# A two-layer fp32 block on one core: the last feed-forward multiplies both parts of x in one 512-column product

## The chip, the cores and the metric

The kernel runs on one core of a Trainium2 chip. The metric is the device time of one execution in microseconds, the median of several runs. The core's engines work side by side, each through its own queue in order: TensorE (PE; its weight loads have a row of their own, PEld), VectorE (DVE), ScalarE (ACT), GpSimd (POOL) and SyncE (SP, which issues the DMA transfers). They meet at semaphores.

## The reference

The reference is a two-layer model, then a second two-layer model on its output, all in fp32, with 256 tokens (272 with 16 meta tokens in front) and a width of 1024. What the change touches is one feed-forward, the last of the first model (layer 1, `ffn2`), on 256 tokens:

```python
D_MODEL, SEQ, D_FF = 1024, 256, 2816

def swiglu(h, w_gu, w_down):
    g, u = jnp.split(h @ w_gu, 2, axis=-1)
    return (jax.nn.silu(g) * u) @ w_down

f = swiglu(rms_norm(h, ln_ffn2[i, 0]), ffn2_w_gu[i], ffn2_w_down[i])
h = h + 0.5 * rms_norm(f, ln_ffn2[i, 1])
```

Around it stand three other feed-forwards (on 272 tokens), a convolution mixer and an attention mixer before it, and a recurrent and another attention mixer after it.

## The kernel before

**Layout.** Features lie on the partitions, tokens in the columns. The hidden state H is 8 tiles (KT) of 128 features by 272 tokens. A weight is a block of 128 x 128.

**Split products.** Products are made in fp32r. To keep fp32 accuracy each operand is split in a high part, rounded to fp32r, and a low part, the remainder: `xh`, `xl` for x, `hh`, `hl` for the hidden layer, `wh`, `wl` for the weights. `mm3` makes three products per weight into the same columns of a PSUM bank: wh x xh (line 290), wh x xl (line 291), wl x xh (line 292). In the last feed-forward each has 256 columns, half a bank.

**Weights.** All weights come from one stream (`Weights`): 201 DMA transfers of 16 blocks, issued by SP. A unit is 8 blocks. For each unit ACT casts the raw blocks to `wh` (line 160, 6 buffers) and VectorE subtracts to make `wl` (line 165, 5 buffers). `take` hands out block after block; at the first block of unit u it issues the cast of unit u + 4 and the subtraction of unit u + 3, so these stand in the queues of ACT and VectorE at that place. The order of instructions on each engine is the order of the program.

**The feed-forward (`ffn`).** The gate and the up projections have 22 column tiles (FT) each. Each is one `dense` call of 8 weights, that is one unit. The first four (gate and up of j = 0 and 1) are made together by `dense_group`, weight row by weight row, because x still arrives from the preceding boundary, one feature tile after another. Then the loop over j = 2 to 21: product pg (gate, in a bank `acc`), a step of side work, product pu (up, in a bank `m`), then `part1(j)` and `part2(j - 1)`:

- `part1`: VectorE multiplies pg by r (the inverse norm) to `f1`; ACT takes silu of it to `f2`; POOL multiplies `f2` by r.
- `part2`: VectorE multiplies `f2` by pu to `f3`; ACT copies that to `hh`; VectorE subtracts to make `hl`.

At j = 2 the parts of j = 0 and 1 come too, in the order part1(0), part1(1), part2(0), part1(2), part2(1). After the loop ACT loads another table, and part2(21) follows. The first two of `part1`, `part2` read PSUM on VectorE (rows `f<-acc` and `f<-f,m`).

**Side work.** `side_step` advances a modulation computed from `ada_w_2`: in one step POOL multiplies a piece `aw` of 1024 columns by `cond`, in the next ACT sums it. In this feed-forward it runs up to about j = 17.

**Down.** Eight products of 22 weights each (`dense` with `hh`, `hl`). `post_tile` takes each: ACT squares it for the norm (`sq`) and copies it scaled (`fs`), POOL adds up the squares. Then `boundary` sums the squares by a product with ones and makes the next x, with idle bf16 products (`warm`, line 287) in between.

PSUM has four banks with tag `acc` and four with `m`.

Of the kernel before, what the change touches and what calls it, by code (L numbers as in the profile page):

```python
# [10 lines left out]
F32R = mybir.dt.float32r  # L11
BF16 = mybir.dt.bfloat16
U32 = mybir.dt.uint32
AF = mybir.ActivationFunctionType
# [4 lines left out]
P = 128  # L19
D = 1024  # L20
KT = D // P
NMETA = 16
T = 272
TX = 256
DFF = 2816
FT = DFF // P
# [6 lines left out]
ROW = 320  # L33

AT = {"x1": 16, "h1": 0, "xc": 16, "x2": 12, "h2": 4, "x3": 20, "h3": 48, "xa": 16, "x4": 0, "h4": 0, "xe": 16, "xo": 16}
# [156 lines left out]
def build(tc, nc, ap, stop=99):  # L192
    V, A, G, PE, S = nc.vector, nc.scalar, nc.gpsimd, nc.tensor, nc.sync
    mult, add, sub = ALU.mult, ALU.add, ALU.subtract
# [4 lines left out]
    def tt(e, out, a, b, op):  # L199
        e.tensor_tensor(out=out, in0=a, in1=b, op=op)  # L200
# [10 lines left out]
    def table(f):  # L211
        if f in sets and loaded[0] != sets[f]:
            loaded[0] = sets[f]
            A.preload_act_table_set(sets[f])

    def act(out, a, f, **k):
        table(f)
        A.activation(out=out, in_=a, func=f, **k)  # L218
# [3 lines left out]
    with glob as gp, psp as ps, tc.tile_pool(name="tmp", bufs=2) as tp, tc.manual_schedule():  # L222

        def acc(tag="acc"):
            return ps.tile([P, 512], F32, tag=tag, name=tag)
# [4 lines left out]
        def tmp(tag, n=T, dt=F32, bufs=2, pool=None):  # L230
            return (pool or tp).tile([P, n], dt, tag=tag, name=tag, bufs=bufs)
# [2 lines left out]
        cv = gp.tile([P, CV.n], F32, name="cv")  # L234
        ct = gp.tile([P, CT.n], F32, name="ct")
        H = gp.tile([P, KT, T], F32, name="H")
        xparts = [gp.tile([P, KT * ROW], F32R, name=n) for n in ("xh", "xl")]
        xh = xl = None

        def rows(t, a, n):  # L240

            return t.rearrange("p (k t) -> p k t", t=ROW)[:, :, a : a + n]

        def place_x(a):
            nonlocal xh, xl
            xh, xl = (rows(t, a, T) for t in xparts)

        fs = bp.tile([P, KT, T], F32, name="fs")
        W = Weights(nc, gp, ap["wst"])
# [32 lines left out]
        def warm(n):  # L282

            if n:
                p = acc("m")
                for _ in range(n):
                    PE.matmul(p[:, :256], idle[:, :P], idle, start=True, stop=True)

        def mm3(out, w, a, b, start, stop):
            PE.matmul(out, w[0], a, start=start, stop=False)  # L290
            PE.matmul(out, w[0], b, start=False, stop=False)  # L291
            PE.matmul(out, w[1], a, start=False, stop=stop)  # L292
# [121 lines left out]
        def post_tile(st, p, k, tok, gpost):  # L414
            st.add(p, k == KT - 1)
            act(fs[:, k, tok], p, AF.Copy, scale=gpost[:, k : k + 1])

        def boundary(st, tok, gpre, last=False, prologue=False, dst=None, at=None):
            if at is not None:
                place_x(at)  # L420
# [64 lines left out]
        def pre_rstd(pre, n, direct=False):  # L485
            return rstd(pre.sums(), n, D, 1e-6, eps6, tag="rpre", direct=direct)

        active = []

        def slot():  # L490
            for g in list(active):
                if next(g, 1) == 1:
                    active.remove(g)

        def dense(keys, rhs, n, tag="acc"):

            p = acc(tag)[:, :n]
            for k, key in enumerate(keys):
                a, b = rhs(k)
                mm3(p, W.take(key), a, b, k == 0, k == len(keys) - 1)  # L500
                if k == 3 and active:
                    slot()
            return p

        def dense_group(keysets, rhs, n, order=None, tags=("acc",) * 4):

            pl = [acc(tags[i])[:, :n] for i in range(len(keysets))]
            nk = len(keysets[0])
            order = order or list(range(nk))
            for i, k in enumerate(order):  # L510
                a, b = rhs(k)
                if i:
                    for p, keys in zip(pl, keysets):
                        mm3(p, W.take(keys[k]), a, b, False, i == nk - 1)
                else:

                    ws = [W.take(keys[k]) for keys in keysets]
                    for part in range(2):
                        for p, w in zip(pl, ws):
                            PE.matmul(p, w[part], a, start=part == 0, stop=False)  # L520
                    for p, w in zip(pl, ws):
                        PE.matmul(p, w[0], b, start=False, stop=False)
                if active:
                    slot()
            return pl

        def xrhs(tok):
            return lambda k: (xh[:, k, tok], xl[:, k, tok])

# [10 lines left out]
        def side_step():  # L540
            if side:
                try:
                    next(side[0])
                except StopIteration:
                    side.popleft()


        def ffn(i, name, tok, pre, gpost, between=None, at=0):
            n = tok.stop - tok.start
            with tc.tile_pool(name="ffn", bufs=1) as fp:  # L550
                hh, hl = (rows(fp.tile([P, FT * ROW], F32R, name=m), at, n) for m in ("hh", "hl"))
                gu = lambda half, j: [(f"{name}_w_gu", i, k, half * FT + j) for k in range(KT)]
                x = xrhs(tok)
                state = {}

                def part1(j, pg, pu):
                    t1 = tmp("f1", pool=bp)[:, :n]
                    tt(V, t1, pg, r, mult)
                    s = tmp("f2", pool=bp)[:, :n]
                    act(s, t1, AF.Silu)  # L560
                    tt(G, s, s, r, mult)
                    state[j] = (s, pu)

                def part2(j):
                    s, pu = state.pop(j)
                    hid = tmp("f3", pool=bp)[:, :n]
                    tt(V, hid, s, pu, mult)
                    act(hh[:, j], hid, AF.Copy)
                    tt(V, hl[:, j], hid, hh[:, j].bitcast(F32), sub)

                first = dense_group([gu(0, 0), gu(1, 0), gu(0, 1), gu(1, 1)], x, n, tags=("acc", "m", "acc", "m"))
                for j in range(2, FT):
                    pg = dense(gu(0, j), x, n)
                    if i or name == "ffn2" or j >= 8:
                        side_step()
                    if j == 2:
                        r = pre_rstd(pre, n, True)
                    pu = dense(gu(1, j), x, n, "m")
                    if j == 2:
                        part1(0, first[0], first[1])  # L580
                        part1(1, first[2], first[3])
                        part2(0)
                    part1(j, pg, pu)
                    part2(j - 1)
                if between is None:
                    table(ARS)
                part2(FT - 1)
                st = Stats(n)
                for m in range(KT):
                    if m == 1 and between:  # L590
                        between()
                        table(ARS)
                    p = dense([(f"{name}_w_down", i, k, m) for k in range(FT)], lambda k: (hh[:, k], hl[:, k]), n)
                    if m == KT - 1:
                        W.ahead()
                    post_tile(st, p, m, tok, gpost)
                    if m < KT - 1:
                        side_step()
                return st
# [14 lines left out]
        def conv(pre):  # L614
            tok = slice(0, T)
            with tc.tile_pool(name="conv", bufs=1) as cp:
                oh, ol = (rows(cp.tile([P, KT * ROW], F32R, name=m), 0, T) for m in ("oh", "ol"))
                ub = [cp.tile([P, T + 2], F32, name=f"ub{j}") for j in range(2)]
                for u in ub:
# [235 lines left out]
        x2 = lambda k: (xh[:, k, :N2], xl[:, k, :N2])  # L855
# [515 lines left out]
        full, tok = slice(0, T), slice(NMETA, T)  # L1371
# [103 lines left out]
def program(stop=99):  # L1475
    import concourse.bacc as bacc

    nc = bacc.Bacc("TRN2", target_bir_lowering=False, num_devices=1)
    shapes = {
        "xT": (P, KT, T),  # L1480
        "cvec": (P, CV.n),
        "ctab": (P, CT.n - P),
        "ctab2": (P, CT2.n),
        "ada": (2, 24, P, D),
        "crep": (P, D),
        "poolw": (P, 4, P),
        "wst": (NCHUNK, P, SUB * P),
    }
    ap = {n: nc.dram_tensor(n, s, F32, kind="ExternalInput").ap() for n, s in shapes.items()}
    ap["out"] = nc.dram_tensor("out", (P, KT, TX), F32, kind="ExternalOutput").ap()  # L1490
    with tile.TileContext(nc) as tc:
        plan = build(tc, nc, ap, stop)
    return nc, plan
# [11 lines left out]
```

## Time and profile before

| | us |
|---|---|
| median of 3 runs | 1362.07 |
| lowest, highest | 1360.29, 1367.23 |
| the profiled execution's own time | 1369.89 |
| its span, first to last instruction | 1367.9 |

| engine | busy us | share of the span |
|---|---|---|
| PE | 1326.6 | 97% |
| PEld | 1288.2 | 94% |
| DVE | 1037.2 | 76% |
| ACT | 753.7 | 55% |
| POOL | 497.0 | 36% |

The mean granted TensorE clock is 0.993 of full speed. Matmuls are pipelined in the profile: the duration of one (0.28 us) is longer than the distance to the start of the next, so the pace of PE is read from starts. L290 is line 290 of the kernel before; `acc<-xh,wh` means that `acc` is written and `xh` and `wh` are read. The helpers at lines 197, 200, 204, 206 and 218 hold most VectorE, POOL and ACT operations, so rows are told apart by their tiles. The last feed-forward runs from 877.94 to 1068.3 us of the span; its loop over j ends about 1006.

### The profile page before, as it was taken

The page shows a single profiled execution, that of the slowest core. Times are in us where ns is not written, and L with a number is a line of the kernel's source. Part 1 is how long each engine was busy: PE and PEld are TensorE (multiplying, and loading weights), DVE is VectorE, ACT ScalarE, POOL GpSimd, SP SyncE. Part 2 cuts the span into 40 slices and gives each one's busy share as a digit, 9 for nine tenths or more (in the row PEclk, how much of TensorE's full clock was granted, in tenths as well). Part 3 has the DMA queues.
Part 4 walks back from the last instruction along what each step waited for, and adds up shares of the span by engine and source line. Part 5 has one row for each costly group of instructions (what it writes and reads, how often), then busy time and mean ns, then how long its engine had stood idle before and what let it go on. Part 6 is the DMA issues. An engine that isn't in the chain of part 4 may idle for free.

```text
span 1367.9 us, 25743 instructions
## 1 busy us (share of the span) xinstructions
PE 1326.6 (97%) x10458; PEld 1288.2 (94%) x10458; DVE 1037.2 (76%) x1505; ACT 753.7 (55%) x1314; POOL 497.0 (36%) x460
## 2 busy tenths in 40 slices
PE   8999999999999999999999998999999989999998
PEld 8999998998999998999998887899999889899888
DVE  6778558878898547988647877788854797877885
ACT  6555544455565545655545555665654546657663
POOL 2133223444333223432224775443200347523420
PEclk9999999999999999999999999999999999999999
DMA  7666663563666562676652332356655332454321
GB/s 251 241 225 221 227 216 97 209 209 133 214 249 231 217 216 109 216 246 207 218 194 95 139 105 93 124 200 240 229 210 185 129 124 97 153 183 155 124 93 62
DMA packets 39286, 242.23 MB, mean 177 GB/s; under 512 B 4352, under 2 KB 5888, under 8 KB 13696
## 3 DMA queue, kind: packets, MB, share of 16 engines
q1 hardware_dynamic: 39168, 240.59, 50.5%
q8 instruction: 82, 1.34, 0.4%
q14 instruction: 36, 0.29, 0.1%
HBM read 239.53 MB, written 1.05 MB: 176 GB/s over the span
## 4 chain that ended last, share of the span: by engine, by line
PE 73%; DVE 17%; POOL 5%; ACT 2%; issue 2%; DMA 0%; SPq 0%; POOLq 0%; ACTq 0%; DVEq 0%
PE acc L291 16%; PE acc L290 16%; PE acc L292 16%; PE m L292 7%; PE m L290 7%; PE m L291 7%; DVE wl L165 4%; DVE H L200 2%; DVE xl L197 1%; POOL rs L200 1%; DVE bt L197 1%; DVE ex L204 1%; POOL hx L200 1%; ACT wh L160 1%; DVE ev L200 1%
## 5 line engine op out<-in xcount | busy, mean ns | idle before, releaser
L165 DVE TENSOR_TENSOR wl<-raw,wh 128x1024 fp32r<-128x1024 f32 x400 | 587.8, 1492 | 132.9 <-ACT wh L160 75.1
L160 ACT CAST wh<-raw 128x1024 fp32r<-128x1024 f32 x400 | 407.1, 1041 | 46.5 <-PE acc L291 21.5
L290 PE MATMUL acc<-xh,wh 128*128 128x272 f32 (+2 forms) x1361 | 400.2, 294 | 2.7 <-ACT wh L160 1.9
L291 PE MATMUL acc<-xl,wh 128*128 128x272 f32 (+2 forms) x1361 | 393.2, 289 | 1.8 <-DVE xl L197 1.7
L292 PE MATMUL acc<-xh,wl 128*128 128x272 f32 (+2 forms) x1361 | 389.4, 286 | 0.6 <-DVE wl L165 0.6
L291 PEld LDWEIGHTS acc<-xl,wh 128*128 128x128 f32 x1361 | 259.6, 191 | 11.0 <-DVE xl L197 7.9
L290 PEld LDWEIGHTS acc<-xh,wh 128*128 128x128 f32 x1361 | 258.9, 190 | 8.5 <-issue 2.2
L292 PEld LDWEIGHTS acc<-xh,wl 128*128 128x128 f32 x1361 | 259.0, 190 | 1.0 <-DVE wl L165 0.9
L292 PE MATMUL m<-xh,wl 128*128 128x272 f32 (+2 forms) x855 | 245.2, 287 | 1.3 <-DVE wl L165 1.2
L290 PE MATMUL m<-xh,wh 128*128 128x272 f32 (+2 forms) x855 | 246.3, 288 | 0.0
L291 PE MATMUL m<-xl,wh 128*128 128x272 f32 (+2 forms) x855 | 244.7, 286 | 0.0
L290 PE MATMUL acc<-hh,wh 128*128 128x272 f32 (+1 forms) x704 | 201.9, 287 | 0.0
L291 PE MATMUL acc<-hl,wh 128*128 128x272 f32 (+1 forms) x704 | 201.9, 287 | 0.0
L292 PE MATMUL acc<-hh,wl 128*128 128x272 f32 (+1 forms) x704 | 201.9, 287 | 0.0
L200 POOL TENSOR_TENSOR sacc<-sacc,sq 128x272 f32<-128x272 f32 (+1 forms) x92 | 83.8, 911 | 291.9 <-ACT sq L218 274.3
L200 POOL TENSOR_TENSOR f<-f,rpre 128x272 f32<-128x272 f32 (+1 forms) x88 | 67.2, 765 | 315.6 <-ACT f L218 315.6
L292 PEld LDWEIGHTS m<-xh,wl 128*128 128x128 f32 x855 | 161.8, 189 | 2.0 <-DVE wl L165 1.9
L291 PEld LDWEIGHTS m<-xl,wh 128*128 128x128 f32 x855 | 162.4, 190 | 0.3
L290 PEld LDWEIGHTS m<-xh,wh 128*128 128x128 f32 x855 | 161.9, 189 | 0.3
L218 ACT ACTIVATE f<-f 128x272 f32<-128x272 f32 (+1 forms) x88 | 37.3, 428 | 180.7 <-DVE f L200 180.7
L291 PEld LDWEIGHTS acc<-hl,wh 128*128 128x128 f32 x704 | 133.6, 190 | 0.0
L292 PEld LDWEIGHTS acc<-hh,wl 128*128 128x128 f32 x704 | 132.9, 189 | 0.0
(377 smaller groups left out, 2062.8 us busy)
## 6 DMA issues: line engine op xcount, KB each, us to landing
raw<-wst SPq DMA_DIRECT2D x199, 1024.0 KB, 4.9
aw<-ada SPq DMA_DIRECT2D x48, 512.0 KB, 5.7
raw<-wst SPq DMA_DIRECT2D x3, 512.0 KB, 8.8
out<-H SPq DMA_DIRECT2D x8, 128.0 KB, 1.9
H<-xT SPq DMA_DIRECT2D x3, 272.0 KB, 8.0
raw<-wst SPq DMA_DIRECT2D x2, 256.0 KB, 3.6
cond<-crep SPq DMA_DIRECT2D x1, 512.0 KB, 5.7
cnt<-ctab SPq DMA_DIRECT2D x1, 512.0 KB, 3.7
```

Source lines behind the costliest of these rows:

```text
L160: self.nc.scalar.copy(self.h[u], r)
L165: self.nc.vector.tensor_tensor(out=self.l[u], in0=r, in1=self.h[u].bitcast(F32), op=ALU.subtract)
L197: V.scalar_tensor_tensor(out=out, in0=a, scalar=s, in1=b, op0=op0, op1=op1, **k)
L200: e.tensor_tensor(out=out, in0=a, in1=b, op=op)
L204: e.tensor_scalar(out=out, in0=a, scalar1=s1, scalar2=None, op0=op0)
L218: A.activation(out=out, in_=a, func=f, **k)
L290: PE.matmul(out, w[0], a, start=start, stop=False)
L291: PE.matmul(out, w[0], b, start=False, stop=False)
L292: PE.matmul(out, w[1], a, start=False, stop=stop)
```

## The change

In the feed-forward whose two parts fit in 512 columns (`pair`: 2 x 256, the last one alone), the high and the low part of x lie in one tile, and so do those of the hidden layer, whose rows get 256 columns instead of 320. `mm2` replaces `mm3`: one product wh x [xh | xl] of 512 columns fills both halves of a bank, and one product wl x xh of 256 columns adds to the first half. In the first four products the first weight row is still done in products of 256 columns. Whoever reads a product first adds its halves (`one`): ACT copies the second half to a tile in SBUF, VectorE adds the first half to it. This comes before the multiplication by r in `part1`, before the hidden product in `part2`, and before `post_tile` for each down product. The other three feed-forwards keep `mm3`.

```diff
+        def mm2(out, w, a, ab, start, stop):
+
+            PE.matmul(out, w[0], ab, start=start, stop=False)
+            PE.matmul(out[:, 0], w[1], a, start=False, stop=stop)
...
+        def dense2(keys, rhs, tag="acc"):
+
+            p = halves(tag)
+            for k, key in enumerate(keys):
+                mm2(p, W.take(key), *rhs(k), k == 0, k == len(keys) - 1)
+                if k == 3 and active:
+                    slot()
+            return p
+
+        def halves(tag):
+            return acc(tag).rearrange("p (s t) -> p s t", s=2)
+
+        def dense_group2(keysets, rhs, tags):
+            pl = [halves(t) for t in tags]
+            nk = len(keysets[0])
+            for k in range(nk):
+                a, ab = rhs(k)
+                ws = [W.take(keys[k]) for keys in keysets]
+                if k == 0:
+
+                    for part in range(2):
+                        for p, w in zip(pl, ws):
+                            PE.matmul(p[:, 0], w[part], a, start=part == 0, stop=False)
+                    for p, w in zip(pl, ws):
+                        PE.matmul(p[:, 1], w[0], ab[:, 1], start=False, stop=False)
+                else:
+                    for p, w in zip(pl, ws):
+                        mm2(p, w, a, ab, False, k == nk - 1)
+            return pl
...
-                hh, hl = (rows(fp.tile([P, FT * ROW], F32R, name=m), at, n) for m in ("hh", "hl"))
+
+                pair = 2 * n <= 512
+                w = n if pair else ROW
+                hparts = fp.tile([P, 2 * FT * w], F32R, name="h").rearrange("p (s c) -> p s c", s=2)
+                hh, hl = (rows(hparts[:, q], at, n, w) for q in range(2))
...
+                def one(p, tag):
+
+                    if not pair:
+                        return p
+                    t = tmp(tag, TX, pool=fp)
+                    act(t, p[:, 1], AF.Copy)
+                    tt(V, t, t, p[:, 0], add)
+                    return t
...
                 def part1(j, pg, pu):
                     t1 = tmp("f1", pool=bp)[:, :n]
-                    tt(V, t1, pg, r, mult)
+                    tt(V, t1, one(pg, "g"), r, mult)
                     s = tmp("f2", pool=bp)[:, :n]
                     act(s, t1, AF.Silu)
                     tt(G, s, s, r, mult)
...
                 def part2(j):
                     s, pu = state.pop(j)
                     hid = tmp("f3", pool=bp)[:, :n]
-                    tt(V, hid, s, pu, mult)
+                    tt(V, hid, s, one(pu, "u"), mult)
                     act(hh[:, j], hid, AF.Copy)
                     tt(V, hl[:, j], hid, hh[:, j].bitcast(F32), sub)
...
-                    p = dense([(f"{name}_w_down", i, k, m) for k in range(FT)], lambda k: (hh[:, k], hl[:, k]), n)
+                    keys = [(f"{name}_w_down", i, k, m) for k in range(FT)]
+                    p = one(dense2(keys, h2), "d") if pair else dense(keys, lambda k: (hh[:, k], hl[:, k]), n)
```

## Rows read from the trace of the kernel before

**Rows 1.** The page's first part: busy us, share of the span, instructions of each engine.
```profile
PE 1326.6 (97%) x10458; PEld 1288.2 (94%) x10458; DVE 1037.2 (76%) x1505; ACT 753.7 (55%) x1314; POOL 497.0 (36%) x460
```

**Rows 2.** Stretches of the last feed-forward; the first line names the columns.
```profile
core 0: us, PE busy (x) PEld busy (x) DVE busy (x) ACT busy (x) POOL busy (x), PEclk, DMA share, GB/s
...
907.00:980.00 73.00, 72.30 (x616) 72.10 (x615) 65.90 (x70) 42.86 (x69) 28.16 (x21) 1.00 0.70 243
...
1006.00:1069.00 63.00, 63.00 (x536) 62.87 (x535) 28.86 (x27) 28.81 (x40) 5.84 (x8) 1.00 0.54 184
```

**Rows 3.** PE in order of time (start, duration, engine, instruction), 36 starts apart.
```profile
984.76 0.28 PE L290 MATMUL acc<-xh,wh 128*128 128x256 f32 x1
...
989.00 0.28 PE L290 MATMUL acc<-xh,wh 128*128 128x256 f32 x1
```

**Rows 4.** VectorE in order of time, two steps of the gate/up loop.
```profile
945.57 0.41 DVE L200 TENSOR_TENSOR f<-acc,rpre 128x256 f32<-128x256 f32 x1
945.90 0.40 DVE L200 TENSOR_TENSOR f<-f,m 128x256 f32<-128x256 f32 x1
946.83 0.75 DVE L200 TENSOR_TENSOR hl<-f,hh 128x256 fp32r<-128x256 f32 x1 [0.53 <-ACT hh L218]
947.50 2.35 DVE L165 TENSOR_TENSOR wl<-raw,wh 128x1024 fp32r<-128x1024 f32 x2
949.77 0.41 DVE L200 TENSOR_TENSOR f<-acc,rpre 128x256 f32<-128x256 f32 x1
...
956.14 0.41 DVE L200 TENSOR_TENSOR f<-acc,rpre 128x256 f32<-128x256 f32 x1
```

**Rows 5.** POOL's groups by line from 907 to 975: count, busy us, mean ns.
```profile
L200 POOL TENSOR_TENSOR aw<-aw,cond 128x1024 f32<-128x1024 f32 x7 | 18.1, 2587 | 0.0
```

**Rows 6.** ACT in order of time, the same steps.
```profile
946.07 0.42 ACT L218 ACTIVATE f<-f 128x256 f32<-128x256 f32 x1 [3.79 <-DVE f L200]
946.39 0.40 ACT L218 ACTIVATE hh<-f 128x256 fp32r<-128x256 f32 x1
...
947.64 1.05 ACT L218 ACTIVATE aw<-aw 128x1024 f32<-128x1024 f32 x1
...
948.69 1.03 ACT L160 CAST wh<-raw 128x1024 fp32r<-128x1024 f32 x1
```

**Rows 7.** VectorE in order of time, a weight split late in the loop.
```profile
979.24 1.21 DVE L165 TENSOR_TENSOR wl<-raw,wh 128x1024 fp32r<-128x1024 f32 x1
```

**Rows 8.** PE in order of time, the first product that uses that split.
```profile
986.41 0.28 PE L292 MATMUL m<-xh,wl 128*128 128x256 f32 x1
```

**Rows 9.** PE in order of time: a 384-column product, its successor, fourteen idle products.
```profile
1273.67 0.34 PE L1268 MATMUL m<-nc,sel 128*128 128x384 f32 x1
1273.85 0.38 PE L1269 MATMUL m<-qk,oqz 128*128 128x128 f32 x2
...
1069.47 1.69 PE L287 MATMUL m<-idle 128*128 128x256 bf16 x14
```

**Rows 10.** POOL in order of time, multiplications of silu by r.
```profile
901.14 1.43 POOL L200 TENSOR_TENSOR f<-f,rpre 128x256 f32<-128x256 f32 x2 [5.80 <-ACT f L218]
...
946.56 0.73 POOL L200 TENSOR_TENSOR f<-f,rpre 128x256 f32<-128x256 f32 x1 [3.14 <-ACT f L218]
```

**Rows 11.** VectorE in order of time at j = 2.
```profile
900.20 0.75 DVE L200 TENSOR_TENSOR f<-acc,rpre 128x256 f32<-128x256 f32 x2
901.92 0.42 DVE L200 TENSOR_TENSOR f<-f,m 128x256 f32<-128x256 f32 x1 [0.97 <-POOL f L200]
902.82 0.42 DVE L200 TENSOR_TENSOR hl<-f,hh 128x256 fp32r<-128x256 f32 x1 [0.48 <-ACT hh L218]
```

**Rows 12.** ACT in order of time: the end of the loop, the last down product.
```profile
1004.60 1.28 ACT L214 ACT_TABLE_LOAD   x1
...
1068.41 0.39 ACT L218 ACTIVATE sq<-acc 128x256 f32<-128x256 f32 x1 [1.96 <-PE acc L292]
```

**Rows 13.** PE in order of time, the first down product's 22nd weight.
```profile
1013.38 0.28 PE L290 MATMUL acc<-hh,wh 128*128 128x256 f32 x1
```

**Rows 14.** The waits from 878 to 1070: who for whom, us, times, longest.
```profile
PEld acc L291 <- DVE xl L197: 1.5, 6, 0.5
```

## What the change should do to the time

> **What bounds the kernel now.** I read the page's busy shares first, then the last feed-forward by stretches, then its engines in order of time. Over the span TensorE is busy 97% and VectorE 76% [rows 1], but that is a mean. In the last feed-forward PE is full at granted clock 1.00, the 2.4 GHz level; VectorE is busy 65.9 of the 73 us from 907 to 980, and 28.9 of the last 63 [rows 2]. So there is room on VectorE in the down products, and little in the gate/up loop.
>
> PE starts a 256-column product every 0.1178 us (36 starts in 4.24 us), so a weight of three products takes 0.353 us, a unit of eight weights 2.83, and two steps j of the gate/up loop (four units) 11.31 [rows 3]. VectorE goes through two steps in 10.57 us (945.57 to 956.14), idle in them only for the two waits of about 0.5 us for ACT's hh [rows 4]. Its order in a step is: two `wl` splits, the gate product times r, the hidden product of the step before, its low part `hl`. The other engines alternate two kinds of step: in one POOL multiplies an `aw` piece for 2.59 us [rows 5], which stretches VectorE's step from 4.20 to 6.37 [rows 4]; in the other ACT sums that piece for 1.05 us [rows 6]. `wl` is made three units ahead of its use, so VectorE's lead over PE is what decides. It grows by 11.31 - 10.57 = 0.74 us in two steps. The `wl` begun at 979.24 lasts 1.21 and is first used at 986.41 [rows 7, 8]: 5.96 us of lead. Seven pairs of steps before, it was 5.96 - 7 x 0.74 = 0.8: nothing to spare at the start.
>
> **The change part by part.** *PE.* Each of 528 weights loses one product of 256 columns and one weight load; one product of 512 columns replaces two of 256. No row shows a 512-column product of this type. The nearest: 256 columns 0.1178 us [rows 3], 384 columns 0.18 [rows 9], that is 0.46 and 0.47 ns per column: time goes with columns, and I take 512 columns at 0.236 us, twice 0.1178, a gain of nothing. From below, the bf16 idle products of 256 columns start every 0.109 us, (1.69 - 0.28)/13 [rows 9]; twice that is 0.218, 18 ns less per weight and 9.5 us over 528. From above, the 0.18 is at most 0.19 as rounded, and 128 columns more at its 0.072 give 0.262, 26 ns more per weight.
>
> The Trainium skill, "TensorE: Matmul & The Clock Gate", section Back-to-back issue gap, puts the warm gap at N/2.4 + 2.5 ns. That would be 216 ns for 512 columns and 109 for 256, so 325 per weight instead of 353, and 15 us off over 528 weights. The bf16 row agrees with it [rows 9]; the rows of this type do not (118 against 109 at 256 columns, 180 against 162 at 384 [rows 3, 9]), and by them the gain is about zero.
>
> *The two halves added on the way out.* Every gate, up and down product now passes an ACT copy of its second half and a VectorE add before its old reader. What they cost lies in their place in two queues that run in the program's order. In a step ACT does copy g, silu, copy u (of the step before), hh; VectorE does add g, multiply by r, add u, hidden product, `hl`. Copy u stands behind the silu, the silu behind VectorE's multiply, and VectorE's add u waits for copy u. Starts, from [rows 4, 6]: a VectorE operation follows the one before it by 0.34; silu starts 0.50 after the multiply (945.57 to 946.07); the next ACT operation 0.32 later; VectorE 0.44 after the start of the ACT operation that it waits for (946.39 to 946.83). So from multiply to hidden product it is 0.50 + 0.32 + 0.44 + 0.34 = 1.60, where now it is 0.33: 1.27 more, and 0.34 for add g. POOL's `f` multiply starts 0.49 after silu and lasts 0.73 [rows 10]. Now it falls on `hl`, whose two inputs lie in SBUF and which takes 0.75 beside it [rows 4] and 0.42 without (902.82) [rows 11]; a multiply with one input from PSUM keeps 0.42 beside POOL (901.92, with POOL busy from 901.14 for 1.43) [rows 10, 11]. Afterwards it falls into the wait: 0.32 back, less 0.10 for the hidden product, which loses its PSUM input. Sum per step: 1.27 + 0.34 - 0.32 + 0.10 = 1.39 us.
>
> By kind of step: where ACT sums a piece, its second cast starts 2.30 after hh (946.39 to 948.69) and the next operation 0.95 after that [rows 6]; so copy g starts 3.25 and add g 3.69 after hh began. VectorE would be ready at 0.44 + 2.94 - 0.32 = 3.06 (949.77 - 946.83 [rows 4], without the collision). That adds 0.63: 4.20 + 1.39 + 0.63 = 6.2. In the `aw` step the piece begins right behind `f`, while VectorE waits about 0.5 us for hh, and so takes about 0.5 us less from it than the 2.17 of now: 6.37 + 1.39 - 0.5 = 7.3. Two steps: 13.5 us, against PE's 11.31. The lead cannot grow; VectorE sets the pace. Bounds: 12.6 if the wait for copy g vanishes and the `f` collision costs nothing, 14.4 if none of the `aw` loss is spared and every add is hit as well.
>
> *Sum, against the profiled run.* Entry: three gate chains and two hidden ones stand in a row from 900.20 [rows 11]. With the starts above, the first hidden product comes at 903.8 (now 901.92), the second at 907.2, and the next `wl` starts at 908.5. Then seven pairs (seven `aw` pieces [rows 5]): 908.5 + 7 x 13.5 = 1003.0, where now stands 979.24 [rows 7]: 23.8 later, of which the lead of 5.96 absorbs its part. Steps 17 to 20, of which only the first has a sum: 6.2 + 3 x 5.6 = 23.0, so step 21 starts at 1026.0. From there: two `wl` 2.27 (949.77 - 947.50), add g 0.34, 2.2 to hh(20); then ACT's table load of 1.28, which now lies in idle time [rows 12], stands between hh(20) and copy u(21): `hl`(21) is ready after 8.5, at 1034.5. PE, given its `wl` up to 1028.4, is by about 1032 at the 22nd weight of the first down product, which needs it, and waits. That weight starts at 1013.38 today [rows 13]: 21.1 late. In the down products VectorE is under half busy [rows 2], so one add per 7.8 us hides; without that cover it would be 8 x 0.34 = 2.7 us. Last, ACT's square after the final down product, at 1068.41 [rows 12], gets the copy and the add in front of it, 0.44 + 0.49 = 0.9, beside nothing. Sum: 21.1 + 0 + 0.9 = 22.0 us.
>
> The first four products cost the same: PE waits there six times for `xl` from VectorE [rows 14], and the columns per k stay the same. No transfer is added or moved.
>
> The profiled run took 1369.89 us (span 1367.9 and 2 around it), 7.8 above the median of 1362.07; with the sum it gives 1392. I take the difference to hold for either, so the predicted time is 1362.07 + 22.0 = 1384. Own range: pairs -6 to +6, the 512-column product -3 (down stage alone, 176 x 18 ns) to +6, rounding and spread of the runs +-3: 1373 to 1398.
>
> **The rivals.** *Faster: PE keeps the pace.* If a 512-column product pays one fixed cost where two paid two, a weight costs 335 ns, and 9.5 - 0.9 = 8.6 us go: 1353. For it: PE is at 97% [rows 1]. Against: it decides only while two steps of VectorE stay under 32 x 0.335 = 10.7 us, and they take 10.57 before anything is added [rows 4]. By the page's gap this rival would end at 1348. *About the same: the adds cost their own time alone*, with every copy ready: two steps 10.57 + 4 x 0.34 = 11.93, entry 1.7; 23.8 becomes 11.2, less the lead of 5.96, and 0.9: +6, 1368. Against: ACT's order, copy u behind silu. *Dearer: a 512-column product loses* (it does not do what it says): at 0.262 PE sets the pace in the steps without `aw` (16 x 0.38 = 6.1 against 5.6, five of them, +2.5) and in the down stage (176 x 26 ns, +4.6): 1391, or 1398 with the upper bound of the pairs.
>
> **How the numbers follow.** Forecast 1384: 0.74. PE keeps the pace, 1353: 0.07. Adds alone, 1368: 0.11. Dearer, 1391 to 1398: 0.08. The range 1366 to 1400 leaves out the first rival and the tails. Within 0.5% (6.8 us), about what a measurement of this kernel can tell from no change, lies only the adds alone: faster 0.07, same 0.11, slower 0.82.
>
> **What would show it.** Two steps in 13 to 14 us on VectorE between 910 and 1005; idle time of VectorE in front of the add for u, about 0.9 us each, put down to ACT's copy; PE's idle time in the gate/up loop put down to `wl`; 512-column products 0.23 to 0.24 us ahead of their successors; the down products back at full PE. It is wrong if PE shows no waits for `wl` after 915, or if the add for u starts right behind the multiply.

## The result, and the profile after

The changed kernel takes 1399.08 us (median of 6 runs, 1397.20 to 1403.07), the kernel before beside it 1367.61 (6 runs, 1360.29 to 1369.14): a ratio of 1.0241, interval 1.0215 to 1.0266, so 29 to 36 us slower. The forecast was 1384, range 1366 to 1400. The direction came out. The time lies in the range, near its upper end, and 1 us above the prediction's own range, 1373 to 1398. The size did not come out: 22 us forecast, about 32 measured.

The profiled run of after took 1398.24 us, its span is 1396.5. Four starts on PE divide the stage: its first product, the first down product, the last down product, the first product of the stage after it.

| us | first product to first down product | down products | tail | stage |
|---|---|---|---|---|
| before | 877.94 to 1005.96: 128.02 | 62.07 | 1068.03 to 1072.98: 4.95 | 195.04 |
| after | 876.42 to 1029.21: 152.79 | 64.89 | 1094.10 to 1100.61: 6.51 | 224.19 |

The stage is 29.15 us longer. The rest of the span is 1172.9 before and 1172.3 after: nothing was lost outside. Of the 29.15, the gate/up loop has 24.8, the down products 2.8, the tail 1.6.

The page's first part of after (compare [rows 1]): 524 fewer products on PE, 52 more operations each on VectorE and ACT.

```profile
PE 1334.8 (96%) x9934; PEld 1270.0 (91%) x9934; DVE 1053.6 (75%) x1557; ACT 770.6 (55%) x1366; POOL 498.2 (36%) x460
```

Stretches of after (the loop, the down products; compare [rows 2]):

```profile
core 0: us, PE busy (x) PEld busy (x) DVE busy (x) ACT busy (x) POOL busy (x), PEclk, DMA share, GB/s
...
907.00:980.00 73.00, 62.69 (x322) 52.99 (x323) 56.33 (x73) 39.77 (x74) 19.17 (x15) 0.93 0.50 180
...
1050.00:1094.00 44.00, 44.00 (x251) 38.22 (x250) 19.86 (x20) 20.81 (x31) 5.89 (x6) 1.00 0.55 193
```

PE, full in the loop before, is busy 62.7 of 73 us; VectorE's busy time in the same stretch fell from 65.9 to 56.3. No engine is full there: the time goes by waits between engines. VectorE of after in order of time, two steps of the loop (compare [rows 4]):

```profile
946.98 0.42 DVE L200 TENSOR_TENSOR f<-g,rpre 128x256 f32<-128x256 f32 x1
948.21 0.42 DVE L200 TENSOR_TENSOR u<-u,m 128x256 f32<-128x256 f32 x1 [0.81 <-ACT u L218]
948.74 0.43 DVE L200 TENSOR_TENSOR f<-f,u 128x256 f32<-128x256 f32 x1
949.65 0.42 DVE L200 TENSOR_TENSOR h<-f,h 128x256 fp32r<-128x256 f32 x1 [0.48 <-ACT h L218]
949.99 2.35 DVE L165 TENSOR_TENSOR wl<-raw,wh 128x1024 fp32r<-128x1024 f32 x2
952.85 0.42 DVE L200 TENSOR_TENSOR g<-g,acc 128x256 f32<-128x256 f32 x1 [0.51 <-ACT g L218]
953.31 0.42 DVE L200 TENSOR_TENSOR f<-g,rpre 128x256 f32<-128x256 f32 x1
954.49 0.42 DVE L200 TENSOR_TENSOR u<-u,m 128x256 f32<-128x256 f32 x1 [0.76 <-ACT u L218]
955.02 2.63 DVE L200 TENSOR_TENSOR f<-f,u 128x256 f32<-128x256 f32 x1
958.13 0.43 DVE L200 TENSOR_TENSOR h<-f,h 128x256 fp32r<-128x256 f32 x1 [0.48 <-ACT h L218]
...
961.19 0.43 DVE L200 TENSOR_TENSOR f<-g,rpre 128x256 f32<-128x256 f32 x1
```

From multiply to multiply the step in which ACT sums a piece takes 6.33 us (946.98 to 953.31, before 4.20), the step with an `aw` piece 7.88 (953.31 to 961.19, before 6.37). A pair takes 14.21 us where PE, unhindered, needs 11.3. Every add for u waits about 0.8 us for ACT's copy. In the second step the hidden product lasts 2.63 us; POOL shows what runs beside it:

```profile
954.96 2.40 POOL L200 TENSOR_TENSOR aw<-aw,cond 128x1024 f32<-128x1024 f32 x1
```

The waits of after from 878 to 1105 (who for whom, us in total, times, longest):

```profile
PE m L297 <- DVE wl L165: 17.5, 8, 3.6
...
PE acc L296 <- DVE h L200: 2.5, 1, 2.5
```

So PE waits eight times for a low part of the weights in the loop, and once, at the first down product, for the last low part of the hidden layer. In the down products it then runs without a gap, one weight (a 512-column and a 256-column product) every 0.353 us: twelve weights in 4.24 us, the time of 36 products before [rows 3].

```profile
1049.70 0.40 PE L296 MATMUL acc<-h,wh 128*128 128x512 f32 x1
...
1053.94 0.40 PE L296 MATMUL acc<-h,wh 128*128 128x512 f32 x1
```

### The profile page after: what moved, and what is told of

Its sections match the earlier page's. It is cut to its first block, busy times and chain, and to the rows that moved or that the text cites. A ratio compares the mean times of both kernels' runs of the same rounds, so it can differ in the third digit from the quotient of the medians.

```text
span 1396.5 us, 24838 instructions
## 1 busy us (share of the span) xinstructions
PE 1334.8 (96%) x9934; PEld 1270.0 (91%) x9934; DVE 1053.6 (75%) x1557; ACT 770.6 (55%) x1366; POOL 498.2 (36%) x460
## 5 line engine op out<-in xcount | busy, mean ns | idle before, releaser
L300 PE MATMUL acc<-x,wh 128*128 128x272 f32 (+2 forms) x1187 | 350.8, 296 | 1.4 <-ACT wh L160 0.9
L301 PE MATMUL acc<-x,wh 128*128 128x272 f32 (+2 forms) x1187 | 342.5, 289 | 0.6 <-DVE x L197 0.6
L302 PE MATMUL acc<-x,wl 128*128 128x272 f32 (+2 forms) x1187 | 340.2, 287 | 1.1 <-DVE wl L165 1.1
L300 PEld LDWEIGHTS acc<-x,wh 128*128 128x128 f32 x1187 | 226.2, 191 | 6.5 <-issue 2.5
L301 PEld LDWEIGHTS acc<-x,wh 128*128 128x128 f32 x1187 | 226.1, 190 | 6.5 <-DVE x L197 3.4
L302 PEld LDWEIGHTS acc<-x,wl 128*128 128x128 f32 x1187 | 225.8, 190 | 1.5 <-DVE wl L165 1.5
L300 PE MATMUL m<-x,wh 128*128 128x272 f32 (+1 forms) x681 | 197.0, 289 | 0.0
L302 PE MATMUL m<-x,wl 128*128 128x272 f32 (+1 forms) x681 | 195.8, 288 | 0.2 <-DVE wl L165 0.2
L301 PE MATMUL m<-x,wh 128*128 128x272 f32 (+1 forms) x681 | 195.6, 287 | 0.0
L300 PE MATMUL acc<-h,wh 128*128 128x272 f32 x528 | 152.5, 289 | 0.0
L301 PE MATMUL acc<-h,wh 128*128 128x272 f32 x528 | 152.5, 289 | 0.0
L302 PE MATMUL acc<-h,wl 128*128 128x272 f32 x528 | 152.5, 289 | 0.0
L302 PEld LDWEIGHTS m<-x,wl 128*128 128x128 f32 x681 | 128.8, 189 | 0.4 <-DVE wl L165 0.4
L300 PEld LDWEIGHTS m<-x,wh 128*128 128x128 f32 x681 | 129.0, 189 | 0.3
L301 PEld LDWEIGHTS m<-x,wh 128*128 128x128 f32 x681 | 128.9, 189 | 0.2
```

## The experiments

**The merged products alone.** The halves are not added: the readers take the first half as the whole, so the product of `wh` with the low parts is left out of the result.

```diff
-                    t = tmp(tag, TX, pool=fp)
-                    act(t, p[:, 1], AF.Copy)
-                    tt(V, t, t, p[:, 0], add)
-                    return t
+                    return p[:, 0]
```

> The change without its adds: the 512-column products stay, but every reader takes the first half of the bank alone (the product of the weights' high part with the low part of x is left out of the result). Theory (the 512-column product gains nothing, 0.235 us against twice 0.1178, and all of the loss is the copies and adds on ACT and VectorE): within 4 us of the kernel before, VectorE's steps back at 4.2 and 6.4 us, a lead that grows as before. Rival (PE itself got slower: the wide product, the one-tile layout of x and h, or clock that falls in it): 10 to 30 us slower than before. Rival (the wide product gains and the adds hide it): 5 to 10 us faster.

Measured: 1368.05 us, ratio 1.0023 (1.0002 to 1.0044), against 1365.12 beside it. The stage of its profiled run takes 195.04 us, to the hundredth that of before, and the steps are back at 4.21 and 6.37:

```profile
943.69 0.41 DVE L200 TENSOR_TENSOR f<-acc,rpre 128x256 f32<-128x256 f32 x1
...
947.90 0.41 DVE L200 TENSOR_TENSOR f<-acc,rpre 128x256 f32<-128x256 f32 x1
...
954.27 0.41 DVE L200 TENSOR_TENSOR f<-acc,rpre 128x256 f32<-128x256 f32 x1
```

The merge gains nothing: 0.235 us for 512 columns is two products of 256 at the 0.1178 of the profiled run of before. The 3 us by which it is slower are taken up below.

**The adds alone.** The 512-column product is made as two of 256 again, into the two halves; the halves are added as in the change.

```diff
-            PE.matmul(out, w[0], ab, start=start, stop=False)
+            PE.matmul(out[:, 0], w[0], a, start=start, stop=False)
+            PE.matmul(out[:, 1], w[0], ab[:, 1], start=False, stop=False)
             PE.matmul(out[:, 0], w[1], a, start=False, stop=stop)
```

> The adds without the change's merge: two products of 256 columns into the two halves of the bank in place of the one of 512, everything behind them as in the changed kernel. Theory (adds alone): as slow as the changed kernel, 28 to 36 us over the kernel before, two steps of the loop in 14.2 us on VectorE. Rival (the merged product is part of the loss): less than 20 us over. Rival (the merge gains and hides part of the loss): over 40 us.

Measured: 1396.46 us, ratio 1.0223 (1.0193 to 1.0253); the stage takes 223.39 us, 28.35 more than before. VectorE, from multiply to multiply 6.33 and 7.87:

```profile
949.84 0.42 DVE L200 TENSOR_TENSOR f<-g,rpre 128x256 f32<-128x256 f32 x1
...
956.17 0.42 DVE L200 TENSOR_TENSOR f<-g,rpre 128x256 f32<-128x256 f32 x1
957.36 0.42 DVE L200 TENSOR_TENSOR u<-u,m 128x256 f32<-128x256 f32 x1 [0.76 <-ACT u L218]
957.88 2.62 DVE L200 TENSOR_TENSOR f<-f,u 128x256 f32<-128x256 f32 x1
...
964.04 0.42 DVE L200 TENSOR_TENSOR f<-g,rpre 128x256 f32<-128x256 f32 x1
```

So the loss comes back with the adds alone: the loop takes 152.02 us here and 152.79 in the changed kernel. The down products take 64.87, as in the changed kernel (64.89), but not by the same sum: their products of 256 columns start every 0.1133 us, and behind a wait of PE of 2.17 us the granted clock is 0.66 from 1041 to 1046. What this pace means for the merge is taken up below.

**The order of the copies.** ACT copies u of the step before right behind its copy of g, ahead of the silu. All work is kept; one place in ACT's queue differs.

```diff
+                    t = copied.pop(id(p), None)
+                    if t is None:
+                        t = copy(p, tag)
+                    tt(V, t, t, p[:, 0], add)
+                    return t
+
+                copied = {}
+
+                def copy(p, tag):
                     t = tmp(tag, TX, pool=fp)
                     act(t, p[:, 1], AF.Copy)
-                    tt(V, t, t, p[:, 0], add)
                     return t
...
-                    tt(V, t1, one(pg, "g"), r, mult)
+                    whole = one(pg, "g")
+                    if pair and j:
+                        up = state[j - 1][1]
+                        copied[id(up)] = copy(up, "u")
+                    tt(V, t1, whole, r, mult)
```

> The changed kernel with ACT's copy of the up product's half put ahead of the silu of the same step instead of behind it. Theory (VectorE's add for u waits for a copy that stands behind the silu): the add follows the multiply by 0.34 instead of 1.23 us, so each step loses 0.9, two steps go from 14.2 to 12.4, seven pairs give 12.4 back, the entry 2 and the steps without aw 1.5: 15 to 20 us over the kernel before. Rival (the two adds' own time and their collisions with POOL are the loss, not the queue order): stays at 28 to 36 over, with the idle time only moved.

Measured: 1379.18 us, ratio 1.0097 (1.0062 to 1.0132), 13 to 14 us over the kernel before and a little under the 15 to 20 expected; the stage 206.78. VectorE:

```profile
943.90 0.42 DVE L200 TENSOR_TENSOR f<-g,rpre 128x256 f32<-128x256 f32 x1
944.24 0.41 DVE L200 TENSOR_TENSOR u<-u,m 128x256 f32<-128x256 f32 x1
944.76 0.42 DVE L200 TENSOR_TENSOR f<-f,u 128x256 f32<-128x256 f32 x1
...
946.01 4.57 DVE L165 TENSOR_TENSOR wl<-raw,wh 128x1024 fp32r<-128x1024 f32 x2
...
950.95 0.43 DVE L200 TENSOR_TENSOR f<-g,rpre 128x256 f32<-128x256 f32 x1
```

The add for u starts 0.34 behind the multiply and waits for nothing. In this `aw` step the hidden product is past before the piece begins, and the two `wl` splits are held in its place, 4.57 us for 2.35. The steps are 5.43, 7.05 (943.90 to 950.95, with `aw`) and, without side work, 4.83: 0.8 to 0.9 less in every kind of step. The wait behind the silu is worth that in a step and 17.4 us of the stage (224.19 - 206.78). What is left of a step without `aw` against before, 4.83 - 4.21 = 0.62, is about what two adds take at 0.34 from start to start [rows 4]. The piece still costs 7.05 - 4.83 = 2.22.

**The side work made earlier.** A second side step after each down product of the earlier feed-forwards, so that none is left for this stage.

```diff
                     if m < KT - 1:
                         side_step()
+                        side_step()
```

> The changed kernel with the side work (the aw pieces on POOL and their sums on ACT) advanced twice per down product in the three earlier feed-forwards, so that none of it is left in the last one. Theory (the aw piece holds the hidden product's step for 2.1 us and its sum makes copy g 0.6 late): all steps take 5.7 us, close to PE's 5.65, step 21 starts 19 us earlier than in the changed kernel: 8 to 15 us over the kernel before. Rival (aw only fills time in which VectorE waits anyway): 25 us or more over.

Measured: 1381.82 us, ratio 1.0110 (1.0081 to 1.0140), 15 to 17 us over the kernel before where 8 to 15 were expected; the stage 205.00. Every step is now 5.74 us, wait for u included:

```profile
940.93 0.42 DVE L200 TENSOR_TENSOR f<-g,rpre 128x256 f32<-128x256 f32 x1
942.18 0.42 DVE L200 TENSOR_TENSOR u<-u,m 128x256 f32<-128x256 f32 x1 [0.82 <-ACT u L218]
942.70 0.43 DVE L200 TENSOR_TENSOR f<-f,u 128x256 f32<-128x256 f32 x1
...
946.68 0.43 DVE L200 TENSOR_TENSOR f<-g,rpre 128x256 f32<-128x256 f32 x1
```

So a piece costs 7.88 - 5.74 = 2.14 us in its step and 6.33 - 5.74 = 0.59 in the next. Before, the two kinds of step differed by 2.16: the change spared nothing of the `aw` loss. The down products take 68.07 us here, 6 more than before: PE waits 2.85 us in the first of them (0.35 and 2.50), and behind the second wait it stays for a while at a weight in 0.64 us (stretch 1020 to 1030, granted clock 0.66).

```profile
1020.00:1030.00 10.00, 8.14 (x31) 6.99 (x32) 8.28 (x10) 7.27 (x10) 0.00 (x0) 0.66 0.63 218
...
1021.86 0.80 PE L296 MATMUL acc<-h,wh 128*128 128x512 f32 x1 [2.50 <-DVE h L200]
1022.66 0.63 PE L296 MATMUL acc<-h,wh 128*128 128x512 f32 x1
1023.30 0.63 PE L296 MATMUL acc<-h,wh 128*128 128x512 f32 x1
```

**Both, and the side work alone on the kernel before.** The two edits above together on the changed kernel, and the second side step alone on the kernel before.

> The changed kernel with both: copy of the up half ahead of the silu, and the side work done in the earlier feed-forwards. Theory (queue order and side work are the whole of the loss but for the entry and the tail): VectorE's steps would take 4.9 us, PE's 5.65 sets the pace again, and what is left is the entry (2 us) and the copy and add behind the last down product (1.5 us): 1 to 6 us over the kernel before. Rival (something else, such as the clock or the banks held longer, carries part of it): 8 us or more over.

> The kernel before with the same shift of the side work, as the control of the two runs with it. Theory (there the side work only keeps VectorE's lead small and costs PE the waits for wl of the first steps, 2.4 us together): 0 to 3 us faster than before. Rival (the shift itself gains or costs elsewhere, in the down products that now hold twice the pieces): more than 4 us away from before, and then the runs with it have to be corrected by that much.

Measured: 1372.08 us, ratio 1.0061 (1.0044 to 1.0078), and 1370.61, ratio 1.0028 (1.0002 to 1.0053). Both times miss what was expected: with both edits it is 8.3 us over the kernel before by the ratio, not 1 to 6, which by the time alone is the rival's figure; the kernel before with the shift came out 3.8 us slower by the ratio, not 0 to 3 faster. The stages decide between theory and rival: they take 195.74 and 193.82 us. With both edits VectorE's steps are PE's, two units of 2.83 apart:

```profile
955.34 0.42 DVE L200 TENSOR_TENSOR g<-g,acc 128x256 f32<-128x256 f32 x1 [0.73 <-ACT g L218]
...
960.99 0.42 DVE L200 TENSOR_TENSOR g<-g,acc 128x256 f32<-128x256 f32 x1 [0.73 <-ACT g L218]
```

Order and side work together account for the loop: with both gone the stage is within 0.7 us of before, tail included, and 1.9 us over that of the kernel before with the same shift; 1.6 of it is the tail. Neither kernel beats the one before, though: in these two profiles the rest of the span is longer (1371.3 - 195.7 = 1175.6 and 1368.6 - 193.8 = 1174.8). It is 1175.0 in the third profile with the side work made earlier, and between 1169.2 and 1173.6 in the nine without. Where the earlier side work costs there was not followed.

**The change in the down products alone.** Gate and up as before; the down products merged and added.

```diff
...
-                    tt(V, t1, one(pg, "g"), r, mult)
+                    tt(V, t1, pg, r, mult)
...
-                    tt(V, hid, s, one(pu, "u"), mult)
+                    tt(V, hid, s, pu, mult)
...
-                first = dense_group2(four, x2, tags) if pair else dense_group(four, x, n, tags=tags)
-                product = (lambda keys, tag: dense2(keys, x2, tag)) if pair else lambda keys, tag: dense(keys, x, n, tag)
+                first = dense_group(four, x, n, tags=tags)
+                product = lambda keys, tag: dense(keys, x, n, tag)
```

> The change in the eight down products alone; gate and up as in the kernel before. Theory (VectorE has room there, the wide product gains nothing, and only the copy and add behind the last product are bare): 0.5 to 3 us slower than before. Rival (each of the eight adds holds up the wl behind it until its product ends): 4 to 10 us slower. Rival (with VectorE free, the wide product shows a gain of 18 ns per weight): 2 us faster.

Measured: 1366.08 us, ratio 1.0024 (1.0012 to 1.0037). The adds hide behind PE, which has no gap:

```profile
999.00:1061.00 62.00, 62.00 (x353) 53.91 (x352) 29.60 (x31) 29.89 (x45) 6.75 (x6) 1.00 0.55 187
```

But its loop, the code of before, took 124.53 us, not 128.02, while its merged down products took 62.06. That raised a new question: is the pace of before's products one pace?

**The kernel before again, three times.** Unchanged, one profile each, on the same chip one after the other.

> The kernel before, unchanged, profiled once more, to see what its single executions differ in. The profiled one of the start took 1369.89 us, while most runs of it lie near 1364. Theory (PE takes the 256-column products of the last feed-forward's loop at one of two paces, 0.1135 or 0.1178 us, and the slower one stood in the first profile; the changed kernel does not feel it, since VectorE sets its pace): an execution of 1361 to 1365 us shows that loop in about 124 us, one near 1370 in 128. Rival (the few us come from elsewhere, such as the clock or the start): the loop takes 128 us in all of them.

> The same once more, as a second execution of the unchanged kernel before. Theory (two paces of PE): the loop takes about 124 us if the execution takes 1361 to 1365, 128 if it takes near 1370. Rival (elsewhere): 128 in both cases.

> The same once more, as a third execution of the unchanged kernel before. Theory (two paces of PE): the loop takes about 124 us if the execution takes 1361 to 1365, 128 if it takes near 1370. Rival (elsewhere): 128 in both cases.

| us | loop | down products | tail | stage | run |
|---|---|---|---|---|---|
| before, profiled run | 128.02 | 62.07 | 4.95 | 195.04 | 1369.89 |
| again, first | 124.54 | 59.73 | 4.95 | 189.21 | 1363.36 |
| again, second | 128.03 | 62.07 | 4.95 | 195.05 | 1366.85 |
| again, third | 124.55 | 59.73 | 4.95 | 189.22 | 1361.96 |
| down products alone changed | 124.53 | 62.06 | 6.51 | 193.10 | 1365.13 |

The same products run at one of two paces, 36 starts in 4.24 us [rows 3] or, here in the first of the three, in 4.08 (0.1133 us each), with PE full and the granted clock at 1.00 both times:

```profile
950.09 0.28 PE L290 MATMUL m<-xh,wh 128*128 128x256 f32 x1
...
954.17 0.28 PE L290 MATMUL acc<-xh,wh 128*128 128x256 f32 x1
...
1001.09:1060.82 59.73, 59.73 (x530) 59.73 (x528) 28.83 (x27) 28.20 (x39) 5.30 (x8) 1.00 0.56 194
```

The stage is 5.83 us shorter at the faster one. The merged products of the change, of the merge alone and of the down products alone ran at 0.353 us a weight, which is what three products take at the slower pace. Against the faster one (0.340) the merge therefore loses 0.013 us a weight, (62.06 - 59.73)/176 from the table. This would fit the 3 us of the merge alone, if the runs of before beside it, which have no profile, had either pace.

## Why the prediction was right in direction and short in size

**VectorE takes over the pace: right.** Its steps became longer than PE's, PE waited for `wl` in the loop, the add for u waited 0.8 us for the copy behind the silu, and putting that copy ahead of the silu gave 17.4 us back. The rival in which the adds cost their own time alone is out: it needs the add right behind the multiply, which only the reordered kernel shows. The rival in which PE keeps the pace is out with it, and so is the dearer 512-column product as the main cause: with products of 256 columns the loss stands, and without the adds it is gone.

**The terms, measured from the first product of the stage.**

| us | forecast | measured | more |
|---|---|---|---|
| start of the stage to the `wl` behind the first hidden products | 30.6 (908.5 - 877.94) | 30.9 (907.29 - 876.42) | 0.3 |
| seven pairs | 94.5 | 99.5 (to 1006.83) | 5.0 |
| steps 17 to 20 | 23.0 | 23.5 (to 1030.35) | 0.5 |
| step 21 to the 22nd weight of the first down product | 8.5 | 9.0 (to 1039.35) | 0.5 |
| from there to the last down product | as before, 54.65 | 54.75 | 0.1 |
| tail, added | 0.9 | 1.56 | 0.7 |

The sum of the last column is 7.1, and 22.0 + 7.1 is the 29.15 of the two profiled runs but for rounding. The forecast of 1384 fell 15.1 us short of 1399.08. These 7.1 are one part of it; 5.5 are the kernel before, which has a median of 1367.61 in the comparison and not 1362.07; the remaining 2.4 are what the medians differ by more than the two profiled runs (31.5 against 29.15). The parts of the prediction's own range add up to 1372 to 1399, not 1373 to 1398.

**The step that failed: the `aw` step of the pair.** The prediction had the piece begin while VectorE waits for hh and "so takes about 0.5 us less"; 7.3 us came out as 7.88, the summing step's 6.2 as 6.33, and 0.71 more a pair is the 5.0. The piece begins right behind POOL's multiplication by r, as forecast, but VectorE does not yet wait for hh: the hidden product starts at 955.02, 0.06 behind the piece at 954.96. By the prediction's own starts it stood 1.60 behind the multiply and the piece 0.50 + 0.49 + 0.73 = 1.72, only 0.12 apart; measured are 1.71 and 1.65. The starts were mis-sized: 0.34 between two VectorE operations holds where the second does not need the first (943.90 to 944.24 in the reordered kernel), while from add u to the hidden product it is 0.53 (954.49 to 955.02) and from add g to the multiply 0.46. So the hidden product meets the piece. Before, it read u from PSUM and lasted 0.40 [rows 4]; now u comes from the copy in SBUF, both inputs lie there, and it lasts 2.63 beside the piece and 0.42 to 0.43 without (948.74). The forecast charged the lost PSUM input with 0.10, for POOL's multiplication by r, and nothing for the piece. The Trainium skill, "SBUF — State Buffer", section Who interferes with whom, says that a VectorE instruction with two SBUF inputs contends with a GpSimd instruction that reads SBUF, and that one with at most one (outside its two-port modes) does not; the rows agree. The loss stayed whole (2.14 against 2.16). It does so in the reordered kernel too (2.22), where the hidden product is past before the piece begins (945.74), but VectorE's wait for hh is past as well and the `wl` splits are hit: in neither order does the piece meet an idle VectorE. The copy of g waited behind the sum as forecast (0.59 against 0.63). The 14.21 of the pair lies within the bounds given, 12.6 to 14.4, near the end in which nothing is spared.

**The tail: short by 0.7.** A weight cast now stands in ACT's queue between the copy and the square, which the forecast left out. ACT and VectorE in order of time at the end of after (compare [rows 12]):

```profile
1094.48 0.38 ACT L218 ACTIVATE d<-acc 128x256 f32<-128x256 f32 x1 [4.13 <-PE acc L297]
1094.76 1.04 ACT L160 CAST wh<-raw 128x1024 fp32r<-128x1024 f32 x1
1094.89 0.42 DVE L200 TENSOR_TENSOR d<-d,acc 128x256 f32<-128x256 f32 x1 [4.24 <-ACT d L218]
1095.69 0.42 ACT L218 ACTIVATE sq<-d 128x256 f32<-128x256 f32 x1
```

The square starts 1.59 behind the last product (1094.10), before 0.38 (1068.03 to 1068.41): 1.21 more instead of 0.9. At the 0.50 that a waiting ACT operation takes behind VectorE it would have started at 1095.39, not 1095.69; the cast accounts for the 0.3. From the square to the next stage's product it is 4.92 us (before 4.57), and these 0.35 were not followed. The kernel with the down products alone changed has the same tail, 6.51 us.

**The 512-column product: right in its size, wrong in what it was set against.** 0.236 us was taken, 0.235 came out. The Trainium skill, "TensorE: Matmul & The Clock Gate", section Back-to-back issue gap, would have had 216 ns; no run here shows that for this type, and the measured 235 decide. But "a gain of nothing" holds only against the slower pace, which the profiled run of before happened to have, and "I take the difference to hold for either" joined it to a median of runs that, by their times, include the faster one. After's loop goes by VectorE, so it gains nothing when PE is faster: against a run of before at the faster pace the loss is 224.19 - 189.21 = 35.0 us, against one at the slower pace 29.15. The measured 31.5 between the medians lies between the two. The profiled time of before, 7.8 above the median of the runs shown, was the hint: against the fastest of the three runs again (1361.96) it is 7.9 longer, and 5.8 of that is this stage's.

**Hidden: right.** The adds of the down products cost PE nothing (no gap after 1039.35).

## What to carry to other kernels

Where a product's halves are added by another engine, cost the place of the copy in that engine's queue, not its duration: behind a silu it made VectorE wait 0.8 us a step, ahead of it not at all. List each operation whose input moves from PSUM to SBUF, and what GpSimd does beside it: here one of 0.42 us lasted 2.63. Count such a loss as spared only where the starts show the engine idle with room to spare; a gap of 0.12 us in the forecast turned round. And when the profiled run stands apart from the median, find the stage in which it does before a difference is carried from the one to the other.

## What was not expected of the hardware

The same stream of 256-column products of this type runs at 0.1133 or 0.1178 us each, in runs of one kernel on one chip, with the granted clock at 1.00 in both. The traces show where the pace changes. From about 897 us on, it holds in every profile with such a stream from one stop of PE to the next, and turns only across a stop. In the profiled run of before, 24 starts take 2.72 us (0.1133 each) ahead of PE's second wait for `wl`, and 2.82 (0.1175) behind it:

```profile
909.00 0.28 PE L290 MATMUL acc<-xh,wh 128*128 128x256 f32 x1
...
911.72 0.28 PE L290 MATMUL m<-xh,wh 128*128 128x256 f32 x1
...
912.81 0.39 PE L292 MATMUL m<-xh,wl 128*128 128x256 f32 x1 [0.70 <-DVE wl L165]
913.04 0.28 PE L290 MATMUL m<-xh,wh 128*128 128x256 f32 x1
...
915.86 0.28 PE L290 MATMUL acc<-xh,wh 128*128 128x256 f32 x1
```

From there the slower pace holds to the end of the stage, without a wait. In the first and third of the three runs again it is the other way round: 0.1178 ahead of a stop of PE near 905, 0.1133 behind it to the end of the stage. The kernel with the adds alone stops often, and has both paces. In the kernel with the down products alone changed, PE does not stop between the loop, which has the faster pace, and the merged down products, which take 0.353 us a weight; that merged products have a faster pace as well, no run shows. Which of the two paces a stream has behind a stop stays open.

After some of PE's waits the granted clock fell to its lower level, 1.2 GHz, for some microseconds: after the first of the eight in the loop of after, 3.61 us long, a weight takes 0.64 us instead of 0.353 (granted clock 0.58 from 910 to 912, 1.00 from 912 on).

```profile
904.55 0.40 PE L296 MATMUL m<-x,wh 128*128 128x512 f32 x1
908.56 0.58 PE L297 MATMUL m<-x,wl 128*128 128x256 f32 x1 [3.61 <-DVE wl L165]
908.94 0.63 PE L296 MATMUL m<-x,wh 128*128 128x512 f32 x1
```

In the loop it shows no cost: VectorE's steps stay at 6.33 and 7.88 throughout, and PE waits for them in any case. In the down products it is on the path: the kernel with the side work made earlier lost some 3 us to it behind a wait of 2.50. The changed kernel waited 2.51 us at the same place, and its products went on at 0.35; why the clock fell in the one and not in the other stays open.
